# A two-layer encoder trunk: solved diagonal blocks sent through DRAM in other pieces, the block step's operands and a decay strip made in another order, and own buffers for a reload

## The chip, the cores and the metric

The kernel runs on one core of a Trainium2 chip. The metric is the device time of one launch in microseconds (us). Three runs of the kernel before took 2922.13 us in the median (2919.28 to 2929.7).

## What is computed

Two layers over 528 tokens (16 learned ones and 512 given) of 1024 channels, all in float32. Each layer normalises its input, projects it with one wide matrix, and mixes the tokens in two ways: a gated delta rule with 8 heads of 128 channels, and a retention with 4 heads of 256/512 channels, each run forwards and backwards. Both results are normalised per head, gated, projected up, merged with sigmoid gates, projected, and added to the residual; a SwiGLU network follows. The part that the change touches is the delta rule, whose chunks need a triangular system solved:

```python
m = jnp.einsum('nbhid,nbhjd->nbhij', kb, k) * decay * lower_strict
a = m + jnp.eye(CHUNK, dtype=m.dtype)
u = lax.linalg.triangular_solve(a, v * beta[..., None], left_side=True, lower=True, unit_diagonal=True)
w = lax.linalg.triangular_solve(a, kb * jnp.exp(gc)[..., None], left_side=True, lower=True, unit_diagonal=True)
```

and the retention's decay factors, a power of the distance between two tokens, `exp(rel * log_gamma)`.

## The kernel before, in words

**Matrix work.** `project` (L422) and its generator `units` loop over tiles of 128 output columns. A weight tile of 1024 x 128 (512 KB) is loaded by a DMA (`wraw`, three buffers), split into a rounded part by ScalarE (`whi`, L178) and a rest by VectorE (`wlo`, L179; four buffers each), and multiplied in three passes (`mm3`): 48 matrix products for the two halves of 264 tokens. In the last layer most products need only the 512 given tokens.

**Two streams.** Per layer there are four groups of two delta-rule heads. `gdn_begin` projects q, k and v of a group; `gdn_chain` then solves and scans it. `weave` mixes `gdn_chain`, which is a chain of small steps, with `filling`: retention heads 0 to 2 and gate projections, which keep TensorE busy. When the fourth group's chain runs, the filling ends; retention head 3 and the last gates are traced behind it.

**The solve.** For each head and direction (four per group, `j`) `gdn_products` makes `N`, 4 chunks of 128 x 128 with the chunk's tokens on the partitions (for direction 1 its transpose `NT`). The 32 x 32 diagonal blocks are wanted one per partition: `N` is written whole to a DRAM tile `nd` (L617), and four DMAs (L622) gather 4 blocks each, in pieces of 128 bytes, into 16 partitions of `w0` (called `w` in the profile). The meta tokens' block goes the same way through `ndm` (L624, L625). `gdn_solve` (L646) then inverts all 68 blocks at once on VectorE: 30 steps of a product (`st`) and a sum (`w`). The result is written to the DRAM tile `xd` in one DMA of 68 rows of 4 KB (L660).

**The block step.** `gdn_levels` (L664), once per head, reads its blocks back as `qc` with 128 partitions (L679), copies and transposes them in blocks of 32 (ScalarE L689, L690, L695; VectorE L686), and spreads them over block-diagonal tiles: `T` and `Q` (both `QT` in the profile) and `TT` by VectorE, `Qf` and `Qb` by ScalarE (L125). TensorE's first product `lvy` needs `T`; its next, `lvt`, needs `Q` and the masked result `Y`. Small products for blocks of 64 follow, then the scan `gdn_scan`.

**The decay strip.** `retention` (L933) loads a strip of distances (L936), makes the decay factors on VectorE (`su`, `strip`) and ScalarE (`Exp`), projects q and k, rotates them (`rot`, `ru`), lets its `filler` run, and multiplies the first scores with the strip (`pr`).

**The reload.** After the last scan `load_a` (L1130) reads back, per head, the delta rule's output (`lo<-od_a`), its gate (`lz<-zd`) and a row of inverse roots (`rs<-rsd`), 264 KB each, multiplies them and splits the result (`oh`, `ol`) for the up-projection. All three tiles come from `ctmp`, a ring of six buffers. `load_b` does the same for the retention with the same ring.

**Order.** All data DMAs are issued by SP, in one queue, and an issue that has to wait holds up those behind it. The order of the instructions on each engine is made by a planner: it walks the traced program by priority, with a simulated timeline. `tc.high_priority(offset=...)` moves what is inside ahead: weights by 200 (`PRI`), `load_a` by 1000 (`OA`), `load_b` by 300 (`OB`). The numbers given to `yield` are the shares by which `weave` mixes the streams. On the chip every engine follows its own list in order.

Of the kernel before, what the change touches and what calls it, by code (L numbers as in the profile page):

```python
# [9 lines left out]
F32 = mybir.dt.float32  # L10
F32R = mybir.dt.float32r
I32 = mybir.dt.int32
AF = mybir.ActivationFunctionType
# [5 lines left out]
P = 128  # L19
# [4 lines left out]
L = NM + SEQ  # L24
NC = 4
# [8 lines left out]
SW = L + 400  # L34
# [58 lines left out]
def bc(ap, shape):  # L93
    return ap.to_broadcast(shape)
# [305 lines left out]
def layer(tc, nc, env, l, xn, gd):  # L400
# [124 lines left out]
    def tok(c):  # L525

        return (NM + c * P, P) if c < NC else (0, NM)
# [44 lines left out]
    def gdn_products(h, st):  # L572
        s = st[h]
        hh = h % 2
        q, k = s["q"], s["k"]
        kk, kq, km = ct("kk"), ct("kq"), ct("km")
        for c in range(NCH):
            n0, n = tok(c)
            a = kk[:, c * P:(c + 1) * P] if c < NC else km[0:NM, 0:NM]
            b = kq[:, c * P:(c + 1) * P] if c < NC else km[0:NM, NM:2 * NM]  # L580
            mm(a, k[:, n0:n0 + n], k[:, n0:n0 + n])
            mm(b, k[:, n0:n0 + n], q[:, n0:n0 + n])
        yield 0.4
        s["gr"], s["N"], s["P"], s["Pm"] = [], [], [], []
        cn = st["cn"]
        for d in range(2):
            gr = gp.tile([P, L], F32, name="gcr", tag="gcr", bufs=4)
            nc.sync.dma_start(gr, grow[d * 8 + h:d * 8 + h + 1, :].partition_broadcast(P))
            dd = tp.tile([P, NC, P], F32, name="dd", tag="u", bufs=UB)
            dm = gp.tile([NM, NM], F32, name="dm", tag="dm", bufs=2)  # L590
            mk = cst["maskF"] if d == 0 else cst["maskB"]
            for c in range(NCH):
                n0, n = tok(c)
                o = dd[:, c] if c < NC else dm
                stt(o, gr[0:n, n0:n0 + n], gc[0:n, d, c, h:h + 1], mk[0:n, 0:n], SUB, MIN)
            act(dd, dd, AF.Exp)
            act(dm, dm, AF.Exp)
            yield 1.6
            N = gp.tile([P, NC, P], F32, name="N", tag="NQ", bufs=8)
            Nm = gp.tile([32, 32], F32, name="Nm", tag="Nm", bufs=4)  # L600
            nc.vector.memset(Nm, 0.0)
            Pt = gp.tile([P, NC, P], F32, name="P", tag="P", bufs=4)
            Pm = gp.tile([NM, NM], F32, name="Pm", tag="Pm", bufs=6)
            for c in range(NC):
                stt(N[:, c], kk[:, c * P:(c + 1) * P], cn[:, d, c, hh:hh + 1], dd[:, c], MUL, MUL)
            stt(Nm[0:NM, 0:NM], km[0:NM, 0:NM], cn[0:NM, d, NC, hh:hh + 1], dm, MUL, MUL)
            yield 1.3

            j = hh * 2 + d
            src, srcm = N, Nm  # L610
            if d == 1:
                src = tp.tile([P, NC, P], F32, name="NT", tag="u", bufs=UB)
                nc.vector.transpose(src.rearrange("p c d -> p (c d)"), N.rearrange("p c d -> p (c d)"))
                srcm = gp.tile([32, 32], F32, name="NmT", tag="NmT", bufs=2)
                nc.vector.transpose(srcm, Nm)
            nd = dp.tile([P, NC, P], F32, name="nd", tag="nd", bufs=8)
            nc.sync.dma_start(nd, src)  # L617
            w0 = st["w0"]
            for c in range(NC):
                base = nd[:, c, :]  # L620
                blocks = bass.AP(base.tensor, base.offset, [[32 * NC * P + 32, 4], [NC * P, 32], [1, 32]])
                nc.sync.dma_start(w0[j * 16 + c * 4:j * 16 + c * 4 + 4, :].rearrange("b (r i) -> b r i", r=32), blocks)  # L622
            ndm = dp.tile([32, 32], F32, name="ndm", tag="ndm", bufs=8)
            nc.sync.dma_start(ndm, srcm)  # L624
            nc.sync.dma_start(w0[64 + j:65 + j, :], ndm.rearrange("r i -> (r i)").unsqueeze(0))  # L625
            tt(Pt.rearrange("p c d -> p (c d)"), kq, dd.rearrange("p c d -> p (c d)"), MUL)
            tt(Pm, km[0:NM, NM:2 * NM], dm, MUL)
            s["gr"].append(gr)
            s["N"].append(N)
            s["P"].append(Pt)  # L630
            s["Pm"].append(Pm)
            yield 1.2
# [15 lines left out]
    def gdn_solve(st):  # L648
        w0 = st["w0"]
        w3 = w0.rearrange("p (r i) -> p r i", r=32)  # L650
        nc.gpsimd.memset(w0[:, 0:1024:33], 1.0)
        for q in range(30, 0, -1):
            n = 31 - q
            t = gp.tile([68, 256], F32, name="st", tag="sc", bufs=SB)[:, :q * n].rearrange("p (j i) -> p j i", j=q)
            tt(t, bc(w3[:, 0:q, q:q + 1], [68, q, n]), bc(w3[:, q:q + 1, q + 1:32], [68, q, n]), MUL)
            tt(w3[:, 0:q, q + 1:32], w3[:, 0:q, q + 1:32], t, ADD)
            if q % 2:
                yield 1.05
        xd = dp.tile([68, 1024], F32, name="xd", tag="xd", bufs=2)
        nc.sync.dma_start(xd, w0)  # L660
        st["xd"] = xd
        yield 4.0

    def gdn_levels(h, st):  # L664
# [4 lines left out]
        xd = st["xd"]  # L669
# [5 lines left out]
        qf, tb = comp[:, 0], comp[:, 1]  # L675
        for d, t in enumerate((qf, tb)):
            j = hh * 2 + d
            base = xd[j * 16:j * 16 + 16, :]
# [4 lines left out]
        tm, qm, tl, qb = more[:, 0], more[:, 1], last_[:, 0], last_[:, 1]  # L683

        def turn(o, a, p0, p1):
            nc.vector.transpose(fl(o)[p0:p1], fl(a)[p0:p1])  # L686


        nc.scalar.copy(tm, tb)  # L689
        nc.scalar.copy(qm, qf)  # L690
        for p0 in (0, 64):
            turn(tm, qf, p0, p0 + 32)
            turn(qm, tb, p0, p0 + 32)

        nc.scalar.copy(tl[64:128], tb[64:128])  # L695
        turn(tl, qf, 0, 64)
        turn(qb, tb, 0, P)

        def spread(o, a, m, n):
            tt(o.rearrange("p c (b i) -> p c b i", b=n), bc(a.unsqueeze(2), [P, NC, n, 32]),  # L700
               bc(m.unsqueeze(1).unsqueeze(3), [P, NC, n, 32]), MUL)

        T, Q, Qf, Qb = (gp.tile([P, NC, P], F32, name=n, tag="NQ", bufs=8) for n in ("QT", "QT2", "Qf", "Qb"))
        TT = gp.tile([P, NC, 64], F32, name="TT", tag="sc", bufs=SB)
        spread(T, tm, cst["bm"], 4)
        spread(Q, qm, cst["bm"], 4)
        spread(TT, tl, cst["bm2"], 2)
        for o, a in ((Qf, qf), (Qb, qb)):
            for b in range(4):
                act(o[:, :, b * 32:b * 32 + 32], a, AF.Copy, scale=cst["bm"][:, b:b + 1])  # L710
# [22 lines left out]
        lo, hi = slice(0, 64), slice(64, 128)  # L733
# [129 lines left out]
    def sums(ps):  # L863

        while later:
            later.pop(0)(ps)
# [66 lines left out]
    def retention(h, filler):  # L933
        strip = rp.tile([P, SW], F32, name="strip", tag="strip")
        o0 = COFF["rel"][0]
        nc.sync.dma_start(strip, constd[:, o0:o0 + SW])  # L936
        for a0 in (0, SW // 2):
            sl = slice(a0, a0 + SW // 2)
            u = tmp("su")[:, 0:SW // 2]
            ts(u, strip[:, sl], lgn[:, 8 * l + 4 + h:8 * l + 5 + h], MUL)  # L940
            stt(strip[:, sl], strip[:, sl], lg[:, 8 * l + h:8 * l + h + 1], u, MUL, MIN)
        act(strip, strip, AF.Exp)
        tt(strip[:, 400:400 + P], strip[:, 400:400 + P], ident, ADD)
        rot = []
        for s, (c0, hv) in enumerate(((C_QB, tail), (C_KB, FULL))):
            pre = [tmp("rp0"), tmp("rp1")]
# [4 lines left out]
            r = rp.tile([P, 2, L], F32, name="rot", tag="rot", bufs=2)  # L951
            u = tmp("ru")
            sl = slice(hv[0][0], L)
# [4 lines left out]
            u = tmp("ru")  # L958
# [3 lines left out]
            rot.append(r)  # L962
        q, k = rot
        sums(pt)
        yield from filler
        pr = []

# [148 lines left out]
    bp = bctx.enter_context(tc.tile_pool(name=f"bp{l}", bufs=1, reuse_waits="tile"))  # L1116

    def spread(row):
        r = ctmp("rs")
        nc.sync.dma_start(r[:, t0:L], rsd[row:row + 1, :].partition_broadcast(P))  # L1120
        return r
# [8 lines left out]
    def load_a():  # L1130
        inverse_roots(0, 8)
        res = []
        for h in range(H):
            o, z, rs = ctmp("lo"), ctmp("lz"), spread(h)
            nc.sync.dma_start(o[:, t0:L], od_a[h, :, t0:L])
            nc.sync.dma_start(z[:, t0:L], zd[h, :, t0:L])
            stt(o[:, t0:L], o[:, t0:L], gain[:, 40 + l:41 + l], rs[:, t0:L], MUL, MUL)
            tt(o[:, t0:L], o[:, t0:L], z[:, t0:L], MUL)
            res.append(split_tile(o))
        return [x[0] for x in res], [x[1] for x in res]  # L1140
# [32 lines left out]
    for i in range(8):  # L1173
# [9 lines left out]
        b = xp.tile([P, L], F32R, name="xl", tag="xl", bufs=8)  # L1183
# [99 lines left out]
    for i in range(FT):  # L1283
# [3 lines left out]
        a, b = split_tile(ff[i], i < 9)  # L1287
# [3 lines left out]
    if not last:  # L1291
        nrm = Norm(8 * (l + 1), FULL)
        hs = residual(w_ffn_out[l], (8, 8, 6), (fh, fl_), True, nrm.add, nrm.ready, lambda: nrm.root(0), 1, LF)
        r = boundary(nrm, hs, lambda xs, two, **kw: first_gates(l + 1, xs, two, **kw))
# [75 lines left out]
```

## Time and profile before

| | kernel before |
|---|---|
| median of three runs | 2922.13 us |
| lowest, highest | 2919.28, 2929.7 us |
| the profiled execution | 2919.6 us |
| its span, first to last instruction | 2917.7 us |
| mean granted TensorE clock | 0.987 |
| moved by DMAs, mean rate | 313.48 MB, 107 GB/s |

The span is 1.9 us shorter than the profiled execution's own time. Busy times are in us; PE is TensorE, DVE VectorE, ACT ScalarE, SPq the queue of SyncE, which issues the DMAs. Time stamps count from the first instruction. The part of the profile that follows the chain of work back from the last instruction tells what released each step; a wait is put down to the releaser that came last. A granted clock of 1.00 is 2.4 GHz, 0.50 is 1.2 GHz.

### The profile page before, as it was taken

The numbers are of one execution on the slowest core, as the hardware profiler recorded it, in microseconds if no ns is written. First come the engines' busy times: TensorE is split into PE (matmuls) and PEld (weight loads), VectorE is DVE, ScalarE is ACT, GpSimd is POOL, SyncE is SP. The second block draws the span as 40 slices with busy tenths as digits, with TensorE's granted clock in tenths as the row PEclk, the third lists the DMA queues.
The fourth block names the chain that finished last, engine by engine and source line by source line (L and its number), as shares of the span: only waits on it lengthen the run. The fifth ranks groups of instructions, "written<-read, shape, count | busy, mean of one in ns | idle before, by whom it ended". The sixth has DMA issues, their size and how long they took to land.

```text
span 2917.7 us, 48775 instructions
## 1 busy us (share of the span) xinstructions
PE 2822.1 (97%) x19487; PEld 2579.0 (88%) x19487; DVE 1795.2 (62%) x3854; ACT 1101.0 (38%) x2171; POOL 9.0 (0%) x114
## 2 busy tenths in 40 slices
PE   8999999999999999999999999999997999999998
PEld 8999999999889999999999888888886788888887
DVE  6877858768664545343258779687786564543433
ACT  5444445345333233222234344453443332332222
POOL 0000000000000000000000000000000000000000
PEclk9999999999899999999999999999998999999999
DMA  5433323324245442333444423334241464433332
GB/s 166 112 83 83 100 77 85 99 74 125 70 145 171 137 143 84 91 89 99 123 116 112 107 71 108 88 94 106 71 140 44 154 192 125 130 109 94 92 110 80
DMA packets 506423, 313.48 MB, mean 107 GB/s; under 512 B 55633, under 2 KB 460779, under 8 KB 506195
## 3 DMA queue, kind: packets, MB, share of 16 engines
q1 hardware_dynamic: 506194, 310.36, 37.1%
q8 instruction: 153, 2.51, 0.4%
q14 instruction: 76, 0.61, 0.1%
HBM read 265.28 MB, written 45.02 MB: 106 GB/s over the span
## 4 chain that ended last, share of the span: by engine, by line
PE 84%; DVE 8%; DMA 5%; ACT 2%; issue 1%; SPq 0%; DVEq 0%; ACTq 0%
PE mmps L112 67%; PE rpv L112 3%; PE fu L112 2%; PE oo L112 2%; PE sn L112 1%; DVE wlo L179 1%; PE yy L112 1%; DMA xd<-w 1%; PE ks L112 1%; DMA lo<-od_a 1%; PE rs L112 1%; PE lvy L112 1%; PE lvt L112 1%; DMA lo<-od_b 1%; PE lvq L112 1%
## 5 line engine op out<-in xcount | busy, mean ns | idle before, releaser
L112 PE MATMUL mmps<-xh,whi 128*128 128x264 f32 (+1 forms) x3840 | 1188.0, 310 | 23.7 <-DVE rg L115 12.4
L112 PE MATMUL mmps<-xl,whi 128*128 128x264 f32 (+1 forms) x3840 | 1179.5, 308 | 0.0
L112 PE MATMUL mmps<-xh,wlo 128*128 128x264 f32 (+1 forms) x3808 | 1173.3, 308 | 0.0
L112 PEld LDWEIGHTS mmps<-xh,whi 128*128 128x128 f32 x3840 | 727.2, 189 | 63.2 <-DVE rg L115 14.6
L178 ACT CAST whi<-wraw 128x1024 fp32r<-128x1024 f32 (+1 forms) x392 | 407.3, 1040 | 991.2 <-PE mmps L112 737.0
L179 DVE TENSOR_TENSOR wlo<-wraw,whi 128x1024 fp32r<-128x1024 f32 (+1 forms) x392 | 474.4, 1210 | 485.3 <-ACT whi L178 484.4
L112 PEld LDWEIGHTS mmps<-xl,whi 128*128 128x128 f32 x3840 | 726.2, 189 | 37.0 <-issue 2.9
L112 PEld LDWEIGHTS mmps<-xh,wlo 128*128 128x128 f32 x3808 | 719.9, 189 | 34.3 <-issue 0.5
L112 PE MATMUL mmps<-oh,whi 128*128 128x264 f32 (+2 forms) x1126 | 358.5, 319 | 0.0
L112 PE MATMUL mmps<-oh,wlo 128*128 128x264 f32 (+2 forms) x1126 | 358.1, 318 | 0.0
L112 PE MATMUL mmps<-ol,whi 128*128 128x264 f32 (+2 forms) x1126 | 357.3, 318 | 0.5 <-DVE ol L179 0.4
L112 PEld LDWEIGHTS mmps<-ol,whi 128*128 128x128 f32 x1126 | 211.6, 188 | 16.4 <-DVE ol L179 0.9
L112 PEld LDWEIGHTS mmps<-oh,wlo 128*128 128x128 f32 x1126 | 211.7, 188 | 15.7 <-issue 0.2
L112 PEld LDWEIGHTS mmps<-oh,whi 128*128 128x128 f32 x1126 | 211.5, 188 | 15.0
L115 DVE SCALAR_TENSOR_TENSOR ac<-xc,cw,ac 128x528 f32<-128x528 f32 x192 | 143.6, 759 | 3.4 <-ACT ac L125 0.6
L118 DVE TENSOR_TENSOR ff<-fg,mmps 128x264 f32<-128x264 f32 (+1 forms) x63 | 32.5, 516 | 116.0 <-PE mmps L112 116.0
L112 PE MATMUL rpv<-prh,rv 128*128 128x264 f32 (+1 forms) x384 | 95.5, 323 | 0.0
L118 DVE TENSOR_TENSOR st<-w 68x30 f32<-68x30 f32 (+14 forms) x240 | 78.2, 326 | 19.0 <-DMA w<-ndm 7.1
L118 DVE TENSOR_TENSOR w<-w,st 68x30 f32<-68x30 f32 (+14 forms) x240 | 78.2, 326 | 6.8
L125 ACT ACTIVATE gth<-mmps 128x264 f32<-128x264 f32 (+1 forms) x132 | 59.8, 454 | 57.4 <-PE mmps L112 57.4
L112 PE MATMUL rs<-rot 128*128 128x264 f32 (+3 forms) x240 | 75.1, 456 | 2.8 <-DVE z L115 2.4
L115 DVE SCALAR_TENSOR_TENSOR hn<-mmps,hold 128x264 f32<-128x264 f32 (+2 forms) x51 | 25.4, 498 | 82.6 <-PE mmps L112 76.5
(315 smaller groups left out, 3216.3 us busy)
## 6 DMA issues: line engine op xcount, KB each, us to landing
wraw<-in_w_in_dram SPq DMA_DIRECT2D x194, 512.0 KB
wraw<-in_w_ffn_in_dram SPq DMA_DIRECT2D x88, 512.0 KB
wraw<-in_w_up_b_dram SPq DMA_DIRECT2D x32, 512.0 KB
wraw<-in_w_ffn_out_dram SPq DMA_DIRECT2D x32, 512.0 KB
gcr<-grow SPq DMA_DIRECT2D x32, 264.0 KB
wraw<-in_w_up_a_dram SPq DMA_DIRECT2D x16, 512.0 KB
wraw<-in_w_out_dram SPq DMA_DIRECT2D x16, 512.0 KB
wraw<-in_w_ffn_out_dram SPq DMA_DIRECT2D x16, 384.0 KB
```

What stands on the lines that cost most here:

```text
L112: newest[0] = nc.tensor.matmul(o, lhsT=l, rhs=r, start=start, stop=stop)
L115: (eng or nc.vector).scalar_tensor_tensor(out=o, in0=a, scalar=s, in1=b, op0=op0, op1=op1)
L118: (eng or nc.vector).tensor_tensor(out=o, in0=a, in1=b, op=op)
L125: nc.scalar.activation(o, a, f, **kw)
L178: a = nc.scalar.copy(hi, src)
L179: return a.ins, nc.vector.tensor_tensor(out=lo, in0=src, in1=hi.bitcast(F32), op=SUB).ins
```

## The change

Five edits. The diagonal blocks alone are written to DRAM, by four DMAs, in the order in which `w0` wants them, and come back in one DMA of 16 rows. The solved blocks are written to `xd` by two DMAs, 64 rows and 4 rows. In the block step `T` is made as soon as its transposes are done, and what `Q`, `TT` and `qb` need comes after. The decay strip's arithmetic stands behind the projections of q and k instead of ahead of them; its load stays. In the reload `lo` gets eight buffers of its own (`mrg`, which the gated products use later).

```diff
@@ -613,13 +613,12 @@
-            nd = dp.tile([P, NC, P], F32, name="nd", tag="nd", bufs=8)
-            nc.sync.dma_start(nd, src)
+            nd = dp.tile([16, 1024], F32, name="nd", tag="nd", bufs=8)
+            for b in range(4):
+                o = slice(b * 32, b * 32 + 32)
+                nc.sync.dma_start(bass.AP(nd.tensor, nd.offset + b * 1024, [[32, 32], [4096, NC], [1, 32]]), src[o, :, o])
             w0 = st["w0"]
-            for c in range(NC):
-                base = nd[:, c, :]
-                blocks = bass.AP(base.tensor, base.offset, [[32 * NC * P + 32, 4], [NC * P, 32], [1, 32]])
-                nc.sync.dma_start(w0[j * 16 + c * 4:j * 16 + c * 4 + 4, :].rearrange("b (r i) -> b r i", r=32), blocks)
+            nc.sync.dma_start(w0[j * 16:j * 16 + 16, :], nd)
@@ -657,7 +656,8 @@
         xd = dp.tile([68, 1024], F32, name="xd", tag="xd", bufs=2)
-        nc.sync.dma_start(xd, w0)
+        nc.sync.dma_start(xd[0:64], w0[0:64])
+        nc.sync.dma_start(xd[64:68], w0[64:68])
@@ -685,26 +685,26 @@
-        nc.scalar.copy(tm, tb)
-        nc.scalar.copy(qm, qf)
-        for p0 in (0, 64):
-            turn(tm, qf, p0, p0 + 32)
-            turn(qm, tb, p0, p0 + 32)
-
-        nc.scalar.copy(tl[64:128], tb[64:128])
-        turn(tl, qf, 0, 64)
-        turn(qb, tb, 0, P)
...
+        nc.scalar.copy(tm, tb)
+        for p0 in (0, 64):
+            turn(tm, qf, p0, p0 + 32)
         spread(T, tm, cst["bm"], 4)
+        nc.scalar.copy(qm, qf)
+        for p0 in (0, 64):
+            turn(qm, tb, p0, p0 + 32)
         spread(Q, qm, cst["bm"], 4)
+
+        nc.scalar.copy(tl[64:128], tb[64:128])
+        turn(tl, qf, 0, 64)
         spread(TT, tl, cst["bm2"], 2)
+        turn(qb, tb, 0, P)
@@ -934,13 +934,6 @@
         nc.sync.dma_start(strip, constd[:, o0:o0 + SW])
-        for a0 in (0, SW // 2):
-            sl = slice(a0, a0 + SW // 2)
-            u = tmp("su")[:, 0:SW // 2]
-            ts(u, strip[:, sl], lgn[:, 8 * l + 4 + h:8 * l + 5 + h], MUL)
-            stt(strip[:, sl], strip[:, sl], lg[:, 8 * l + h:8 * l + h + 1], u, MUL, MIN)
-        act(strip, strip, AF.Exp)
-        tt(strip[:, 400:400 + P], strip[:, 400:400 + P], ident, ADD)
         rot = []
@@ -962,6 +955,13 @@
         q, k = rot
         sums(pt)
+        for a0 in (0, SW // 2):
...
+        tt(strip[:, 400:400 + P], strip[:, 400:400 + P], ident, ADD)
         yield from filler
@@ -1131,7 +1131,7 @@
-            o, z, rs = ctmp("lo"), ctmp("lz"), spread(h)
+            o, z, rs = bp.tile([P, L], F32, name="lo", tag="mrg", bufs=8), ctmp("lz"), spread(h)
```

The lines that the fifth hunk adds and that are left out here are those that it removes above, unchanged.

## Rows read from the trace of the kernel before

**Rows 1.** The page's first part: busy us (share of the span) and instructions.
```profile
PE 2822.1 (97%) x19487; PEld 2579.0 (88%) x19487; DVE 1795.2 (62%) x3854; ACT 1101.0 (38%) x2171; POOL 9.0 (0%) x114
```

**Rows 2.** The page's fourth part: the chain that ended last, shares of the span by line.
```profile
PE mmps L112 67%; PE rpv L112 3%; PE fu L112 2%; PE oo L112 2%; PE sn L112 1%; DVE wlo L179 1%; PE yy L112 1%; DMA xd<-w 1%; PE ks L112 1%; DMA lo<-od_a 1%; PE rs L112 1%; PE lvy L112 1%; PE lvt L112 1%; DMA lo<-od_b 1%; PE lvq L112 1%
```

**Rows 3.** Waits of TensorE: waiting for, us in total, times, longest us.
```profile
PE lvy L112 <- DVE QT L118: 21.4, 6, 10.4
PE mmps L112 <- DVE rg L115: 12.4, 8, 4.2
```

**Rows 4.** Timeline of TensorE: start us, us, what, count [idle before <-releaser].
```profile
189.72 0.49 PE L112 MATMUL lvy<-QT,N 128*128 128x128 f32 x2 [0.81 <-DVE QT L118]
...
381.49 0.59 PE L112 MATMUL mmps<-xh,whi 128*128 128x264 f32 x1 [3.34 <-DVE ro L118]
...
578.87 1.01 PE L112 MATMUL lvy<-QT,N 128*128 128x128 f32 x3 [2.63 <-DVE QT L118]
...
763.02 1.16 PE L112 MATMUL lvy<-QT,N 128*128 128x128 f32 x8 [1.43 <-DVE QT L118]
...
775.42 0.98 PE L112 MATMUL lvy<-QT,N 128*128 128x128 f32 x3 [3.04 <-DVE QT L118]
...
2215.39 2.08 PE L112 MATMUL lvy<-QT,N 128*128 128x128 f32 x8 [10.42 <-DVE QT L118]
...
2227.93 2.08 PE L112 MATMUL lvy<-QT,N 128*128 128x128 f32 x8 [3.04 <-DVE QT L118]
```

**Rows 5.** The chain in order of time behind layer 1's fourth solve: start us, us, what.
```profile
2202.62 6.12 DMA xd<-w
...
2209.17 2.13 DMA qc<-xd
```

**Rows 6.** Timeline of VectorE in the same stretch.
```profile
2211.39 0.62 DVE L686 STREAM_TRANSPOSE qd<-qc 32x128 f32<-32x128 f32 x2 [3.42 <-DMA qc<-xd]
...
2214.65 1.29 DVE L118 TENSOR_TENSOR QT<-qd,c_bm 128x512 f32<-128x512 f32 x2
```

**Rows 7.** Busy time by stretch; the first row names the columns.
```profile
core 0: us, PE busy (x) PEld busy (x) DVE busy (x) ACT busy (x) POOL busy (x), PEclk, DMA share, GB/s
...
2204.20:2208.60 4.40, 0.77 (x5) 0.20 (x3) 2.46 (x3) 1.80 (x3) 0.00 (x0) 1.00 0.21 67
380.30:387.10 6.80, 5.61 (x25) 5.61 (x26) 4.22 (x10) 3.34 (x12) 0.00 (x0) 0.50 0.35 111
578.30:581.70 3.40, 2.83 (x13) 2.83 (x14) 2.38 (x4) 2.37 (x6) 0.00 (x0) 0.50 0.22 65
772.90:783.10 10.20, 6.90 (x38) 6.41 (x39) 4.16 (x11) 2.30 (x9) 0.00 (x0) 0.50 0.05 15
2209.90:2223.50 13.60, 7.32 (x40) 6.68 (x40) 5.72 (x14) 4.21 (x14) 0.00 (x0) 0.50 0.30 58
...
831.00:866.00 35.00, 31.09 (x219) 27.63 (x219) 29.62 (x49) 15.90 (x30) 0.00 (x0) 1.00 0.78 241
```

**Rows 8.** The chain in order of time before layer 0's first solve.
```profile
138.55 2.44 DMA nd<-NT
...
142.11 2.09 DMA w<-nd
```

**Rows 9.** Issues of SP: start us, us of the issue, what, count.
```profile
318.41 0.32 SPq L624 DMA_DIRECT2D ndm<-Nm  x1
...
320.23 0.23 SPq L625 DMA_DIRECT2D w<-ndm  x1
```

**Rows 10.** Groups of instructions: busy us, mean ns | idle before, releasers with us.
```profile
L118 DVE TENSOR_TENSOR st<-w 68x30 f32<-68x30 f32 (+14 forms) x240 | 78.2, 326 | 19.0 <-DMA w<-ndm 7.1 <-DMA w<-nd 5.8
...
L115 DVE SCALAR_TENSOR_TENSOR lo<-lo,gain,rs 128x528 f32<-128x528 f32 (+1 forms) x16 | 12.2, 760 | 9.5 <-DMA lo<-od_a 9.4
```

**Rows 11.** Timeline of VectorE inside layer 1's fourth solve.
```profile
2181.13 0.82 DVE L122 TENSOR_SCALAR su<-strip,lgn 128x464 f32<-128x464 f32 x2
...
2182.18 0.69 DVE L115 SCALAR_TENSOR_TENSOR strip<-strip,lg,su 128x464 f32<-128x464 f32 x1
```

More of the change, by code (lines that the diff above doesn't have):

```diff
@@ L964, in retention @@
         sums(pt)
+        for a0 in (0, SW // 2):
+            sl = slice(a0, a0 + SW // 2)
+            u = tmp("su")[:, 0:SW // 2]
+            ts(u, strip[:, sl], lgn[:, 8 * l + 4 + h:8 * l + 5 + h], MUL)
+            stt(strip[:, sl], strip[:, sl], lg[:, 8 * l + h:8 * l + h + 1], u, MUL, MIN)
+        act(strip, strip, AF.Exp)
+        tt(strip[:, 400:400 + P], strip[:, 400:400 + P], ident, ADD)
         yield from filler
```

## The prediction

> **What bounds the kernel now.** I read the page first for the engines: TensorE is busy for 97% of the span [rows 1], and the chain that ended last runs for 67% through the matrix products of `mmps`, while `xd<-w` and `lo<-od_a` have about 1% each [rows 2]. So almost all of the time is matrix work that the change leaves alone; only what TensorE spends idle, or at half its clock, can be won. The waits of TensorE say where that is: its longest is for `QT`, the first operand of the block step (`lvy`), 21.4 us in six waits, then 12.4 us in eight for `rg`, a result of VectorE that stands behind other things in its queue [rows 3]. The third reading is TensorE's timeline around the eight solves. Seven waits belong to them, five in layer 0 and two in layer 1 [rows 4]: in the first three groups of layer 0 (0.81, 3.34, 2.63 us), and in the fourth group of either layer, where little other matrix work is left, one for each of the two heads (1.43 and 3.04; 10.42 and 3.04). The first three groups of layer 1 have none.
>
> What they wait for is in the chain of the last group: the solve ends, `xd<-w` takes 6.12 us, `qc<-xd` 2.13 us [rows 5], then VectorE starts its transposes at 2211.39 and the two `QT` products at 2214.65 [rows 6]. VectorE had stood still for 3.42 us in front of the transposes. In group two of layer 0 TensorE's wait is for `ro` [rows 4], an ordinary product behind that same standstill.
>
> The granted clock is read from stretches: after such a wait TensorE runs at 0.50 of its full clock, the 1.2 GHz level instead of 2.4, for 6.8 us, 3.4 us, 10.2 us and 13.6 us at the four places listed [rows 7]. Work done there takes twice as long.
>
> **The change part by part.** All terms are against the profiled execution, 2919.6 us (span 2917.7); the median of the three runs, 2922.1, stands 2.5 us above it, and I add that at the end.
>
> *xd as 64 and 4 rows* (eight times). The 68 rows move 67 GB/s with a DMA share of 0.21 while they are under way [rows 7], about 3.4 of 16 engines: the transfer is slow because few engines carry it. A tile of 256 KB over 128 rows lands in 2.44 us where nothing is ahead of it [rows 8]. I take 2.9 us for the new pair (2.44, and a second issue of about the 0.3 that an issue takes [rows 9]) instead of 6.12, a gain of 3.2. Bounds: 2.44 and 6.12. The Trainium skill ("DMA: Bandwidth & Descriptors", Why a DMA increments its semaphore by 16 and not by 1) gives the engines as the largest number up to 16 that divides the outer dimensions: 4 for 68 rows, 16 for 64. The share of 0.21 agrees with four. The same page (Rules for kernel authors) advises against splitting a transfer by partitions, since both parts use the same engines; by that rule alone nothing would be won here, and it is the first rival.
> What reaches TensorE is the gain or the wait, whichever is smaller [rows 4]: 3.2 of 3.34, 2.6 of 2.63, 0.8 of 0.81, 1.4 of 1.43, 3.2 of 10.42. **-11.2 us**; bounds -12 and 0. In layer 1's first three groups it is worth nothing, since TensorE has no wait there.
>
> *T first.* Today VectorE does six transposes, two rotary products and `TT` before the first `QT` ends; from 2211.39 to 2214.65 plus half of 1.29 that is 3.9 us [rows 6]. After the change two transposes (0.62) and one product (0.65) stand ahead of `lvy`, 1.3 us: a gain of 2.6 at the wait of 10.42. At the two waits of 3.04 [rows 4] copies for the head before lie in between, so I take 1.8 each. The rest (`Q`, `TT`, `qb`) then runs beside `lvy`, and is next in line to be late: `lvt` needs `Q`. **-6.2 us**; bounds -7.8 and 0 (if the order on VectorE stays as it is).
>
> *The clock.* If the waits of 3.34 and 2.63 go, so does the half clock behind them: half of 5.61 and of 2.83 us of work, 4.2. In the two last groups 6.90 and 7.32 us are worked at half clock [rows 7]; waits remain there, so I take a third of the 7.1 to be had. **-6.6 us**; bounds -11.3 and 0.
>
> *Diagonal blocks alone.* Seven DMAs before (one tile, four gathers, two for the meta block), seven after (four block pieces, one load, the same two). The old path is 2.44 for the tile, then three more issues, then 2.09 for the last gather [rows 8]; the new one is four issues, a landing of the same kind, one issue and a landing. Equal within 0.5 us, and SP waits once in either, with the weight loads queued behind that wait. The solve now waits 12.9 us in all for these loads (7.1 and 5.8) [rows 10]. **0**; bounds -2 and +18 (second rival). What hides it is the work of the other stream; without it the solve starts later by as much.
>
> *Strip late* (eight times). The strip's products on VectorE (0.82, and twice 0.69) lie in the middle of the fourth group's solve in layer 1 [rows 11]. The solve is a chain on VectorE, so its end moves forward by about 2 us in layer 1, where TensorE waits for it. The products go to the wait for `qc`, in which VectorE stands for 3.42 us anyway [rows 6]. The strip's own load stays where it was. **-2 us**; bounds -4 and +3 (if they get in front of the first scores instead).
>
> *Own reload buffers.* VectorE waits 9.4 us for `lo<-od_a` [rows 10]; three heads instead of two can now be under way. But the stretch has a DMA share of 0.78 at 241 GB/s and VectorE is busy for 29.62 of 35 us [rows 7], so little can move. TensorE's waits here are among those for `rg` [rows 3]. **-3 us**; bounds -9.4 and +34 (last rival). The eight `mrg` buffers are next wanted for the gated products after the first up-projection, by which time the reload is read: nothing.
>
> *The new order.* Instructions are ordered by a planner that starts anew; a few waits will appear elsewhere. Three of the size of those for `rg` (12.4 in 8, 1.5 each [rows 3]): **+4.6 us**; bounds 0 and +15.
>
> Sum: -11.2 - 6.2 - 6.6 + 0 - 2 - 3 + 4.6 = -24.4, so 2895.2 in the profiled execution and **2898 us** beside the median.
>
> **The rivals.** About 0.5% (14.6 us) is what a measurement of this kernel can tell from no change, so faster begins under 2907.5.
> *The split of xd wins nothing* (both pieces stay behind the weight loads, or the readers wait for both as long as before, so that the change doesn't do what it says). Against it is the share of 0.21 [rows 7]; for it, that all transfers go through SP's one queue, behind weight tiles of 512 KB. Then the terms for xd and the clock go: 2898 + 17.8 = 2916. Chance 0.13.
> *Short writes.* The blocks now go to DRAM in pieces of 128 bytes instead of 2 KB. If four pieces landed as late as `xd` does today (6.12 instead of 2.44), eight solves would start 3.7 us later; the two last groups and layer 0's other three would pass that on, 18 us: 2916. Against it: `ndm`, pieces of 128 bytes too, was sent at 318.41 and its reader was issued at 320.23 [rows 9], so it had landed within 1.8 us. The Trainium skill (the same page, Specifications) says that transfers below 512 bytes are read, modified and written; by that rule this rival would be the likelier; the trace's 1.8 us shows no such price, though for 32 pieces only. Chance 0.08.
> *The new order eats it.* Ten new waits of 1.5 instead of three: 2898 + 10.9 = 2909. Chance 0.10.
> *The reload pushes out the weights* (the slower side). The reload's loads and products are planned far ahead of everything else; with buffers of their own, nothing holds them back any more. The place is the stretch after the last group's scan. Its 24 transfers of 264 KB are 6.3 MB, 26 us at 241 GB/s. If they all went first, TensorE would have one weight tile in hand, 48 of the 219 matrix products that take 31.09 us there [rows 7], 6.8 us; it would stand for 19 us instead of the 3.9 of now, and 1.5 more at half clock: 16.8 a layer, 34 in all, and the 3 us gained there are lost: 2935. It decides the sign from 11 us a layer on. For it: a DMA share near 0.8; against: today's buffers already let two heads go ahead, and loads of weights still came between. Chance 0.07.
>
> **How the numbers follow.** The forecast has 0.62. Faster: 0.60 of that, and the parts of the third and first rival that stay under 2907.5 (0.05 and 0.03): 0.68. Slower by over 0.5%: the last rival, 0.07. The rest, 0.25, is within it. The low end takes four fifths of the 22 us that the lower bounds (-46.5 in all) leave under the sum: 2880; the high end takes in the first two rivals: 2917.
>
> **What would show it.** Right: `xd` landing under 3.5 us in the chain; the wait of 10.42 down to 2 to 5; those of 3.34 and 2.63 gone with the half clock behind them; about 1.3 us from the first transpose to `lvy`; no strip products inside the solve. Wrong: `xd` still near 6 us; blocks landing after more than 4 us; a wait for `rg` or for weights longer than 4.2 in the reload; more idle time of TensorE outside the solves than 5 us over what is there now.

## The result, and the profile after

The changed kernel takes 2910.89 us in the median of six runs (2908.56 to 2912.14), the kernel before beside it 2927.46 us (six runs, 2919.28 to 2931.21). The ratio is 0.9943, with a 95% interval of 0.9931 to 0.9955: faster by 0.57%. The profiled execution took 2910.8 us, its span 2909.0.

The profile after answers to [rows 1, 2] with these lines of the page: the engines do the same work, and `xd<-w` and `lo<-od_a` are no longer among the largest shares of the chain that ended last.

```profile
PE 2824.6 (97%) x19487; PEld 2581.4 (89%) x19487; DVE 1795.3 (62%) x3854; ACT 1101.5 (38%) x2171; POOL 9.4 (0%) x114
...
PE mmps L112 69%; PE rpv L112 3%; PE fu L112 2%; PE oo L112 2%; PE sn L112 1%; PE yy L112 1%; PE rs L112 1%; DVE wlo L179 1%; PE ks L112 1%; DMA lo<-od_b 1%; DMA gcr<-grow 1%; PE lvy L112 1%; PE lvt L112 1%; PE l64b L112 0%; PE l L112 0%
```

The waits of TensorE after (waiting for, us in total, times, longest us), beside [rows 3]:

```profile
PE lvy L112 <- DVE QT L118: 11.1, 4, 6.1
...
PE mmps L112 <- DVE rg L115: 8.2, 8, 2.7
...
PE rvm L1011 <- DVE pr L118: 5.8, 2, 2.9
```

The first two fell by 14.5 us together; the third, for the product of scores and strip (`pr`), is new among the longer ones. The timeline of TensorE after shows where they lie:

```profile
152.91 0.28 PE L1011 MATMUL rvm<-c_ident,rvc 128*16 128x128 f32 x1 [2.93 <-DVE pr L118]
...
773.92 2.05 PE L112 MATMUL lvy<-QT,N 128*128 128x128 f32 x8 [6.08 <-DVE QT L118]
...
2208.56 1.16 PE L112 MATMUL lvy<-QT,N 128*128 128x128 f32 x8 [0.31 <-DVE QT L118]
...
2218.80 2.05 PE L112 MATMUL lvy<-QT,N 128*128 128x128 f32 x8 [3.52 <-DVE QT L118]
```

Against [rows 4], the wait of 10.42 is down to 0.31, and those of 0.81, 2.63 and 1.43 are gone (3.34 is now 1.19). But one of 2.93 stands at the first solve, and the second head of layer 0's fourth group waits 6.08 where it waited 3.04. The chain of the last group in order of time, beside [rows 5]:

```profile
2199.65 3.38 DMA xd<-w
...
2203.47 2.23 DMA qc<-xd
```

From the issue of `xd` to that of `qc` it is 2.87 to 3.4 us in seven solves and 4.13 in one; before it was 4.9 to 6.2. In the last group a weight tile is still under way when the pair is issued, so the pair is read by itself behind layer 0's third solve: 178 GB/s at a DMA share of 0.80 (67 and 0.21 for the whole in [rows 7]). The other stretches show the half clock gone at the two places of layer 0's second and third group:

```profile
core 0: us, PE busy (x) PEld busy (x) DVE busy (x) ACT busy (x) POOL busy (x), PEclk, DMA share, GB/s
...
572.10:573.60 1.50, 1.50 (x15) 1.50 (x14) 0.00 (x0) 1.07 (x2) 0.00 (x0) 1.00 0.80 178
...
153.30:160.00 6.70, 5.44 (x24) 5.44 (x25) 6.30 (x18) 1.73 (x4) 0.00 (x0) 0.50 0.29 81
...
380.30:387.10 6.80, 5.61 (x47) 5.32 (x47) 5.83 (x12) 4.76 (x16) 0.00 (x0) 1.00 0.42 119
578.30:581.70 3.40, 3.40 (x31) 3.40 (x30) 2.69 (x5) 2.47 (x7) 0.00 (x0) 1.00 0.52 141
```

Instead, 6.7 us at half clock stand behind the new wait at the first solve. VectorE's timeline in the last group, beside [rows 6], is the line that tells most about the forecast:

```profile
2205.79 0.61 DVE L686 STREAM_TRANSPOSE qd<-qc 32x128 f32<-32x128 f32 x2 [0.41 <-DMA qc<-xd]
2206.44 0.50 DVE L686 STREAM_TRANSPOSE qe<-qc 64x128 f32<-64x128 f32 x2
2206.87 0.57 DVE L686 STREAM_TRANSPOSE qd<-qc 32x128 f32<-32x128 f32 x2
2207.47 0.43 DVE L118 TENSOR_TENSOR TT<-qe,c_bm 128x256 f32<-128x256 f32 x1
2207.81 1.29 DVE L118 TENSOR_TENSOR QT<-qd,c_bm 128x512 f32<-128x512 f32 x2
```

All six transposes and `TT` still stand ahead of both `QT` products, as before, and so it is in all 16 heads of the trace after. The text of the kernel put `T` first; the planner's list for VectorE did not. From the first transpose to the end of the first `QT` it is 2.7 us here, where it was 3.9 with two sums of the rotary in between [rows 6]. Layer 0's first solve is later, and VectorE's timeline shows what now stands ahead of it:

```profile
122.03 1.30 DVE L115 SCALAR_TENSOR_TENSOR strip<-strip,lg,su 128x464 f32<-128x464 f32 x2
...
143.08 0.69 DVE L613 STREAM_TRANSPOSE NT<-N 128x512 f32<-128x512 f32 x1
...
151.03 0.20 DVE L118 TENSOR_TENSOR st<-w 68x30 f32<-68x30 f32 x1 [4.67 <-DMA w<-nd]
```

The strip's products of the first retention head are now among the products that make group one's `N`. The same steps in VectorE's timeline before:

```profile
47.04 0.70 DVE L115 SCALAR_TENSOR_TENSOR strip<-strip,lg,su 128x464 f32<-128x464 f32 x1
...
137.02 0.69 DVE L613 STREAM_TRANSPOSE NT<-N 128x512 f32<-128x512 f32 x1
...
144.42 0.20 DVE L118 TENSOR_TENSOR st<-w 68x30 f32<-68x30 f32 x1 [1.16 <-DMA w<-ndm]
```

The last `NT` is 6.1 us later, and the solve that waits for it 6.6. The strip is not all of it: with the strip early again (e3 in the table below) the changed kernel's first solve is still 3.3 us late, and by which edit is open. The strip of the last head of layer 1 now runs behind the whole block step:

```profile
2256.03 1.31 DVE L115 SCALAR_TENSOR_TENSOR strip<-strip,lg,su 128x464 f32<-128x464 f32 x2
```

The new path of the blocks, in the chain before that solve (beside [rows 8]), has landings of the old size:

```profile
146.06 2.81 DMA nd<-NT
...
148.95 1.96 DMA w<-nd
```

From the first issue for the last `NT` to the solve it is 6.5 us, with the four pieces in SP's issues at 144.49, and before it was 5.9 (138.55 to 144.42):

```profile
144.49 2.00 SPq L619 DMA_DIRECT2D nd<-NT  x4
```

The waits of VectorE for the solve's blocks and for the reload, beside [rows 10]:

```profile
L118 DVE TENSOR_TENSOR st<-w 68x30 f32<-68x30 f32 (+14 forms) x240 | 78.2, 326 | 14.2 <-DMA w<-nd 8.2
L118 DVE TENSOR_TENSOR lo<-lo,rs 128x528 f32<-128x528 f32 (+1 forms) x32 | 21.3, 697 | 12.8 <-DMA lo<-od_b 12.8
L115 DVE SCALAR_TENSOR_TENSOR lo<-lo,gain,rs 128x528 f32<-128x528 f32 (+1 forms) x16 | 12.1, 758 | 6.0 <-DMA lz<-zd 5.2 <-DMA rs<-rsd 0.8
```

The wait for `lo<-od_a` is gone, but 5.2 us of it are now for `lz`, the next tile of the same load, which kept the ring of six buffers.

The two profiled executions differ by 8.8 us (that of before, 2919.6 us, is near the low end of its runs). Where these come from is read by following the same instruction through the traces. The table gives, for the profiled execution of each kernel, how much later (+) or earlier (-) than before that instruction starts: the first product of layer 0's first solve; the first up-projection product of layer 0 (the end of its mixing); the first product of layer 1's fourth solve; the first `lvy` there; the first up-projection product of layer 1; the first output product. The kernels are those of the next section.

| | first solve | layer 0 mixed | 4th solve, layer 1 | its lvy | layer 1 mixed | output |
|---|---|---|---|---|---|---|
| before starts at | 144.42 | 895.96 | 2163.02 | 2215.39 | 2339.40 | 2811.53 |
| after | +6.6 | +0.8 | +3.2 | -6.8 | -8.7 | -8.6 |
| e1: blocks by the old path | +7.2 | -0.9 | +2.6 | -6.2 | -3.0 | -1.5 |
| e2: xd whole | +5.9 | +7.9 | +10.8 | +3.5 | +4.3 | +3.2 |
| e3: strip early | +3.3 | -6.1 | -4.8 | -8.5 | -8.9 | -8.9 |
| e4: reload from the ring | +6.7 | +1.2 | +3.5 | -6.8 | -6.4 | -7.8 |
| f1: xd alone | +0.5 | -9.7 | -6.6 | -10.1 | -9.5 | -9.4 |
| f3: strip alone | +6.1 | +4.9 | +6.2 | -0.4 | +0.9 | +1.0 |
| f4: lo alone | +0.6 | +0.7 | +1.9 | +1.4 | +4.6 | +5.0 |
| h1: strip late in the last head | +2.8 | -6.6 | -6.4 | -16.4 | -17.3 | -16.0 |
| f2: T tied | +5.7 | -11.1 | -11.3 | -22.4 | -24.3 | -24.2 |
| h2: both | +1.1 | -10.0 | -8.6 | -19.1 | -20.4 | -18.8 |

So layer 0 gained nothing, and the whole gain was made in layer 1's last group, 10.0 us of it in the 52 us from the start of its solve to `lvy`: 6.1 in the solve (from its first product to the issue of `xd`, 39.6 us before and 33.5 after), 2.7 from there to the issue of `qc`, 1.1 from there to `lvy`. Each column can be read as a difference to its neighbour; a single execution can lie some 7 us off the median of its kernel, so verdicts rest on the medians and ratios, and places on the table, as one execution of each kernel shows them.

### The profile page after: what moved, and what is told of

Its sections match the earlier page's. It is cut to its first block, busy times and chain, and to the rows that moved or that the text cites. A ratio compares the mean times of both kernels' runs of the same rounds, so it can differ in the third digit from the quotient of the medians.

```text
span 2909.0 us, 48823 instructions
## 1 busy us (share of the span) xinstructions
PE 2824.6 (97%) x19487; PEld 2581.4 (89%) x19487; DVE 1795.3 (62%) x3854; ACT 1101.5 (38%) x2171; POOL 9.4 (0%) x114
## 4 chain that ended last, share of the span: by engine, by line
PE 87%; DVE 6%; DMA 3%; ACT 1%; issue 1%; SPq 1%; DVEq 0%; ACTq 0%
PE mmps L112 69%; PE rpv L112 3%; PE fu L112 2%; PE oo L112 2%; PE sn L112 1%; PE yy L112 1%; PE rs L112 1%; DVE wlo L179 1%; PE ks L112 1%; DMA lo<-od_b 1%; DMA gcr<-grow 1%; PE lvy L112 1%; PE lvt L112 1%; PE l64b L112 0%; PE l L112 0%
```

## The experiments

Unless it says otherwise, each is the changed kernel with one part undone or altered; ratios are to the kernel before on the same chip, whose medians were 2922 to 2924 us.

**e1, the blocks by the old path.**

```diff
...
-            for b in range(4):
-                o = slice(b * 32, b * 32 + 32)
-                nc.sync.dma_start(bass.AP(nd.tensor, nd.offset + b * 1024, [[32, 32], [4096, NC], [1, 32]]), src[o, :, o])
+            nc.sync.dma_start(nd, src)
...
```

> The changed kernel with the diagonal blocks sent the old way (whole tile to DRAM, four gathers). Theory: the four block issues per head and direction lengthen SP's list in layer 0's first group, so its solve starts 6.6 us later than before and TensorE waits 3.2 + 1.6 us there; undone, the solve starts at about 144.5 us again instead of 151.0 and the kernel takes 5 to 8 us less than the changed one (2911), about 2904. Rival: the late start comes from the newly planned order as a whole, not from the blocks; then the first solve still starts at 149 to 152 us and the time stays within 3 us of the changed kernel.

2914.03 us (2912.9 to 2917.83), ratio 0.9965 [0.9953, 0.9977]. The first solve starts 7.2 us later than before, as in the changed kernel (6.6): the late start is not the blocks' doing. The 3 us more in the median (6 by the ratios) are barely told apart, since the intervals overlap; in the profile, the slowest of the six executions, they arise behind the last group's first `lvy`. Two waits, of 1.71 and 2.42 us, stand there, and TensorE is at half clock for the 30 us that follow, in which it waits 3.33 us more for the second head:

```profile
2209.19 1.16 PE L112 MATMUL lvy<-QT,N 128*128 128x128 f32 x8 [1.71 <-DVE QT L118]
...
2212.77 2.08 PE L112 MATMUL lvt<-Y,QT 128*128 128x128 f32 x8 [2.42 <-DVE Y L118]
...
core 0: us, PE busy (x) PEld busy (x) DVE busy (x) ACT busy (x) POOL busy (x), PEclk, DMA share, GB/s
2211.40:2242.00 30.60, 25.12 (x138) 21.84 (x139) 13.09 (x36) 8.70 (x28) 0.00 (x0) 0.50 0.10 22
```

**e2, the solved blocks in one DMA.**

```diff
-        nc.sync.dma_start(xd[0:64], w0[0:64])
-        nc.sync.dma_start(xd[64:68], w0[64:68])
+        nc.sync.dma_start(xd, w0)
```

> The changed kernel with xd written in one DMA of 68 rows again. Theory: the split is the larger part of the gain; xd lands in 5 to 6.2 us again instead of 3.2 to 3.4, the waits for the block step in layer 0's second and third group and in the last group come back, and the kernel takes 8 to 13 us more than the changed one, 2919 to 2924. Rival (the gain comes from the new order and from the strip, the transfer is hidden): within 4 us of 2911.

2920.55 us (2916.42 to 2924.53), ratio 0.9991 [0.9982, 0.9999]. Without the split nearly all of the gain is gone. In the issues of SP the reader is 6.19 us behind the write again:

```profile
2207.26 0.28 SPq L659 DMA_DIRECT2D xd<-w  x1
2213.45 0.92 SPq L678 DMA_DIRECT2D qc<-xd  x2
```

**e3, the strip early again** (its arithmetic back behind its load, in all heads).

```diff
         nc.sync.dma_start(strip, constd[:, o0:o0 + SW])
+        for a0 in (0, SW // 2):
...
```

> The changed kernel with the strip's arithmetic back ahead of the projections. Theory: the fourth solve of layer 1, 33.5 us from the first st to xd in the changed kernel and 39.6 before, becomes 2.5 to 6 us longer, and so does the wait behind it: 2913 to 2917. Rival: the solve is shorter for another reason; then it stays near 33.5 us and the time within 2 us of 2911.

2909.2 us (2904.14 to 2910.76), ratio 0.9947 [0.9934, 0.9959]: the same as the changed kernel. The table shows that this is no "nothing": layer 0 ends 6.9 us earlier than with the late strip, and from the fourth solve of layer 1 to its `lvy` 6.3 us of that are lost.

**e4, the reload from the ring.**

```diff
-            o, z, rs = bp.tile([P, L], F32, name="lo", tag="mrg", bufs=8), ctmp("lz"), spread(h)
+            o, z, rs = ctmp("lo"), ctmp("lz"), spread(h)
```

> The changed kernel with lo taken from the ring of six again. Theory: the own buffers let the reload run closer together, which cost as much in layer 0 (waits of 3.1 and 1.5 us before rvm and mmps at 849 to 854 us, half clock behind them) as they won in layer 1 (wait of 2.9 instead of 4.5): within 3 us of 2911. Rival 1 (they win what was forecast): 3 to 6 us more. Rival 2 (they push out the weights in layer 0): 5 us less, and the waits at 849 to 854 us gone.

2911.64 us (2908.51 to 2916.4), ratio 0.996 [0.9948, 0.9973]. Up to the reload it runs like the changed kernel within 0.4 us; at the reload's end it is 0.4 us later in layer 0 and 2.4 in layer 1, and 0.8 at the output. By the ratio it is 5 us behind the changed kernel, by the median 0.8; the intervals overlap.

**f1, the kernel before with the split of xd alone.** The diff is that of e2, turned round.

> The kernel before with xd written in 64 and 4 rows and nothing else changed. Theory: this edit alone carries the gain; xd lands in 3.2 to 3.4 us, the waits of 3.3 and 2.6 us in layer 0's groups two and three and the half clock behind them go, the wait of 10.4 in the last group falls by about 3: 9 to 14 us less than before, ratio 0.995 to 0.997. Rival (it needs the other edits to reach TensorE): ratio 0.998 or more.

2909.36 us (2904.32 to 2910.26), ratio 0.9949 [0.9935, 0.9962]. One line makes as much as all five edits. It gains in layer 0, where the changed kernel gains nothing. TensorE's waits are those that the term for `xd` named: 0.81, 3.34, 2.63 and 1.43 of layer 0 are gone, and 10.42 is 3.2 shorter:

```profile
2205.32 1.01 PE L112 MATMUL lvy<-QT,N 128*128 128x128 f32 x3 [7.20 <-DVE QT L118]
```

**f2, the changed kernel with the order on VectorE tied**: the other transposes and products may be issued only after `T`'s product.

```diff
-        spread(T, tm, cst["bm"], 4)
+        first = spread(T, tm, cst["bm"], 4)
...
+        with tc.issue_after(first):
+            for p0 in (0, 64):
+                turn(qm, tb, p0, p0 + 32)
+            spread(Q, qm, cst["bm"], 4)
...
```

> The changed kernel with VectorE's list tied so that the product for T really stands behind its two transposes (in the changed kernel the planner put it behind all six and TT in all sixteen heads). Theory: from the first transpose to the first lvy it is 1.3 to 1.8 us instead of 2.6 to 8.7; the waits of 6.1 us (layer 0) and 3.5 us (layer 1) for the second heads of the last groups fall by 2 to 4 us each; 4 to 6 us less than the changed kernel, 2905 to 2907, ratio about 0.9925. Rival: lvt then waits for Q instead, and the time stays within 2 us of the changed kernel's.

2902.17 us (2895.19 to 2905.0), ratio 0.9926 [0.9912, 0.994]. VectorE's timeline in the last group now has the order that the change meant:

```profile
2190.71 0.61 DVE L686 STREAM_TRANSPOSE qd<-qc 32x128 f32<-32x128 f32 x2 [0.48 <-ACT qd L695]
2191.36 0.69 DVE L689 TENSOR_TENSOR QT<-qd,c_bm 128x512 f32<-128x512 f32 x1
2191.97 0.61 DVE L686 STREAM_TRANSPOSE qd<-qc 32x128 f32<-32x128 f32 x2
```

`QT` ends 1.34 us after the first transpose starts. Of the table's -24 the median confirms -20; the profiled execution was the quickest of its six. The gain over the changed kernel does not lie where it was forecast: by the table 11.9 of 15.6 us are there at the end of layer 0, and 1.1 are made from the last solve's start to its `lvy`. Some 6 of them are the clock: half clock, summed from the granted clock of 5 us stretches, is 52.2 us against 64.8 in the changed kernel. In layer 0's fourth group the wait of 6.08 is gone, and one of 3.27 stands at the next product:

```profile
771.09 1.16 PE L112 MATMUL lvt<-Y,QT 128*128 128x128 f32 x8 [3.27 <-DVE Y L118]
```

**f3, the kernel before with the late strip alone.**

```diff
-        for a0 in (0, SW // 2):
...
         sums(pt)
+        for a0 in (0, SW // 2):
...
```

> The kernel before with the strip's arithmetic late in every head and nothing else. Theory (late costs some 3 to 4 us before the first solve in layer 0, and is worth something in the last group only where the solved blocks land early): 2923 to 2928 us, ratio 1.000 to 1.002, the first solve 3 to 4 us later than in the kernel before. Rival (late is worth its 2 us or more in the last group of each layer by itself, as forecast): 2916 to 2920 us, ratio 0.998 to 0.999.

2923.36 us (2920.46 to 2928.51), ratio 0.9999 [0.999, 1.0008]. It is two opposite things: the first solve is 6.1 us late, and that is the late strip's work by itself; then layer 1's fourth solve and block step win 6.6 of it back. VectorE's timeline in layer 0 is that of the changed kernel again:

```profile
121.54 1.29 DVE L115 SCALAR_TENSOR_TENSOR strip<-strip,lg,su 128x464 f32<-128x464 f32 x2
...
150.55 0.20 DVE L118 TENSOR_TENSOR st<-w 68x30 f32<-68x30 f32 x1 [4.51 <-DMA w<-ndm]
```

**f4, the kernel before with the own reload buffers alone.** The diff is that of e4, turned round.

> The kernel before with own reload buffers and nothing else. Theory (worth 0 to 3 us): 2919 to 2924 us, ratio 0.999 to 1.000; the waits before the merges at the end of each layer fall by about 2 us. Rival (the earlier reloads stand in front of the weights on the queue and give TensorE a new wait): 2926 to 2935 us.

2924.93 us (2920.69 to 2931.89), ratio 1.0009 [0.9999, 1.0019]. Worth nothing that can be measured; the last rival's 34 us are excluded.

**h1, the strip late in the last head alone.**

```diff
+        def decays():
...
+        if h < RH - 1:
+            decays()
...
         sums(pt)
...
+        if h == RH - 1:
+            decays()
```

> The changed kernel with the strip late for the last retention head only, early for the other three. Theory: late strips of heads 0 to 2 cost, because head 0's falls among the products ahead of the first solve, which started 6.6 us later; that of head 3 wins, because it leaves the last solve. The first solve starts at 145 to 148 us, the last solve takes about 33.5 us, and the kernel takes 4 to 8 us less than the changed one, 2903 to 2907, ratio about 0.992. Rival: the planned order shifts the waits about at random; then within 3 us of 2911 with the first solve's start unchanged.

2898.26 us (2897.36 to 2903.41), ratio 0.992 [0.9907, 0.9932]. By the ratios this is some 7 us better than the changed kernel, with intervals that just touch. Heads 0 to 2 keep layer 0's gain, head 3 keeps the last group's (10.0 us from the last solve's start to `lvy`). TensorE's wait there:

```profile
2198.95 1.16 PE L112 MATMUL lvy<-QT,N 128*128 128x128 f32 x8 [0.25 <-DVE QT L118]
```

**m1, xd as 34 and 34 rows** (a single run).

```diff
-        nc.sync.dma_start(xd[0:64], w0[0:64])
-        nc.sync.dma_start(xd[64:68], w0[64:68])
+        nc.sync.dma_start(xd[0:34], w0[0:34])
+        nc.sync.dma_start(xd[34:68], w0[34:68])
```

> The changed kernel with xd written as two pieces of 34 rows. If the number of engines by the outer dimension sets the time (34 divides by 2 only), the pieces run on two engines each and xd lands in 8 to 10 us, later than the 5 to 6.2 of one piece; if it is two transfers in place of one that wins, xd lands in 3 to 4 us as with 64 and 4.

One run, 2918.38 us. The issues of SP in the last group:

```profile
2202.58 0.26 SPq L659 DMA_DIRECT2D xd<-w  x1
2202.89 0.28 SPq L660 DMA_DIRECT2D xd<-w  x1
2207.49 0.93 SPq L679 DMA_DIRECT2D qc<-xd  x2
2210.14 0.32 SPq L750 DMA_DIRECT2D Qm<-xd  x1
```

`qc` of the first head reads rows 0 to 31, the first piece, and waits 4.91 us for half the bytes. `Qm` reads the meta rows in the second piece, and is issued 7.25 us after it and 2.65 us behind `qc` (1.0 in the kernels before and after, where all of `xd` has landed by then). Once the weight tile ahead of them is through, the two pieces move 52 GB/s at a DMA share of 0.13, about 2 of 16 engines:

```profile
2204.70:2208.40 3.70, 3.70 (x33) 3.70 (x32) 2.46 (x3) 1.32 (x2) 0.00 (x0) 1.00 0.13 52
```

Two pieces of equal size end later than one whole (5 to 6.5 us), though less late than expected. So it is not two transfers in place of one that gains; the shares of 0.21, 0.80 and 0.13 go with the row counts.

**h2, h1 and f2 together.**

> The changed kernel with both repairs: the strip's arithmetic late in the last head alone, and the transposed block product tied to come directly after its own two transposes. Theory (the two lie in different places: the strip of head 0 ahead of group one's first scores in layer 0, the transposed product at the head of every solve and above all of the last): their gains over the changed kernel (2902.17 and 2898.26 against 2910.89, so 8.7 and 12.6 us) add for the most part: 2888 to 2894 us, ratio to before 0.989 to 0.991, the wait before the first product of the transposed solve in the last group near zero. Rival (both gains are the same one, the half clock of the last group that either of them happens to prevent): 2896 to 2902 us, no better than the better of the two.

2897.93 us (2895.57 to 2901.77), ratio 0.9916 [0.9903, 0.9929]. The rival's time is right: no better than h1 (0.992). Its cause, the half clock of the last group, is not shown. What the record shows is that little was left to win where the term put it: the wait before `lvy` in the last group, 0.25 us in h1, is zero, as expected, and TensorE waits just behind it instead:

```profile
2196.32 1.05 PE L112 MATMUL lvy<-QT,N 128*128 128x128 f32 x8
2198.27 1.16 PE L112 MATMUL lvt<-Y,QT 128*128 128x128 f32 x8 [0.90 <-DVE Y L118]
```

In layer 0 the table has h2 3.4 us ahead of h1, and f2 1.1 ahead of h2; the medians of h1 and h2 are the same.

**i1, the kernel before with the split of xd and `T` tied.** The edit puts f2's lines in place of the three old products, but leaves the old copies and transposes standing above them, so these are made twice in every head. It doesn't answer the question that was put to it.

```diff
         turn(tl, qf, 0, 64)
         turn(qb, tb, 0, P)
...
+        nc.scalar.copy(tm, tb)
+        for p0 in (0, 64):
+            turn(tm, qf, p0, p0 + 32)
+        first = spread(T, tm, cst["bm"], 4)
...
```

> The kernel before with the solved blocks sent as 64 and 4 rows and the transposed block product tied behind its own two transposes; diagonal blocks, strip and reload buffers as before. Theory (the pair of moves that shorten one stretch are what counts, the three others are about nothing together): 8 us under the kernel with the 64 and 4 rows alone (2909.36), so 2898 to 2904 us, ratio 0.992 to 0.994. Rival (the tied product gains only beside the other changes): 2907 to 2912 us.

2920.31 us (2915.28 to 2927.57), ratio 0.9988 [0.9979, 0.9997], 11 us above f1. Read for what it is, it prices needless work at this place: the page has VectorE busy for 1820.6 us where f1's has 1796.6, and with these 24.0 us of transposes (and some 11 us of copies on ScalarE, 1113.7 against 1102.3) the kernel is 11 us slower, although VectorE is idle for 38% of the span and `T` is tied. How much the tie gives back in this is not told apart. In the last group `T`'s product starts 3.58 us after the first transpose, behind other transposes and two sums of the rotary:

```profile
2212.37 0.61 DVE L687 STREAM_TRANSPOSE qd<-qc 32x128 f32<-32x128 f32 x2 [0.61 <-DMA qc<-xd]
...
2215.29 0.62 DVE L687 STREAM_TRANSPOSE qd<-qc 32x128 f32<-32x128 f32 x2
2215.95 0.69 DVE L701 TENSOR_TENSOR QT<-qd,c_bm 128x512 f32<-128x512 f32 x1
```

Whether the split and the tied `T` do better alone than h1 was not tried, nor the split with the strip late in the last head.

## Why the forecast held, and where its steps did not

The sign came out, and two thirds of the size (0.9943 against a forecast of 24.4 us less, which is 0.9916), at the slow end of the range. What held is the term for `xd`. That the total stayed in the range is in part luck: the terms for `T`, the strip and the reload, 11.2 us together, brought nothing that can be told from zero, and the 4.6 us set aside for the new order and the width of the range made up for them.

- **xd as 64 and 4 rows** (-11.2): right, and nearly the whole result. The landing of 2.9 us was forecast and 2.87 to 3.4 measured in seven solves. In one solve it was 4.13. Alone (f1) it is worth 13 us; taken away (e2) it leaves 0.1%. In layer 0 it gives -9.7 with the clock, where the four waits and the clock had been put at -8 and -4.2. In the last group, where 3.2 more were forecast, f1 has the `lvy` 3.5 us earlier against the start of the solve, but is only 2.8 better at the end. The first rival (the split wins nothing) fell. The rule behind it in the Trainium skill ("DMA: Bandwidth & Descriptors", Rules for kernel authors) is about two halves that each spread over all 16 engines; the 68 rows, at a share of 0.21, did not, so it does not carry over to them. The same page's rule of the largest divisor (Why a DMA increments its semaphore by 16 and not by 1; 4 for 68, 16 for 64, 2 for 34) agrees with all three shares, 0.21, 0.80 and 0.13: 34 rows by that rule are 17 rows to an engine, as 68 are, and the first piece took 4.91 us against 5 to 6.5.
- **The clock** (-6.6): right in layer 0's second and third group. Over the span, the half clock summed from the granted clock of 5 us stretches is 71.5 us before and 64.8 after, so 3.4 us of time, half of the term. The term counted the half clock that goes and none that comes: new half clock came up at the first solve and in layer 0's reload stretch, 7 us at either. In f1 the same sum is 75.2 us, so `xd` alone gave none back over the span.
- **T first** (-6.2): this step failed. I took "After the change two transposes (0.62) and one product (0.65) stand ahead of `lvy`" from the order of the text; the bound of zero, "if the order on VectorE stays as it is", is what happened: in all 16 heads six transposes and `TT` stand ahead, and in the last group it is 2.7 us from the first transpose to the end of the first `QT`, not 1.3. Whether the order pays as forecast stays open. Tied (f2), it gives 8.7 us by the medians and 5 by the ratios (0.9926 against 0.9943, intervals that overlap a little), near the 6.2, but in the profile it does so in layer 0 and in part through the clock, not at the wait of 10.42; beside h1 it gives nothing (h2). That the wait of 10.42 fell to 0.31 nonetheless was xd and the strip: the stretch from the solve's start to `lvy` got 10.0 us shorter, and alone it is 3.5 in f1 and 6.6 in f3.
- **Strip late** (-2): the wrong size at both places, and the wrong sign at one. The step that failed is "The products go to the wait for `qc`": they do so in none of the eight heads. The last head's run at 2256.03, some 50 us behind that wait. The first head's go in front of group one's blocks, the case of the upper bound, and cost 4.9 us by the end of layer 0 (f3), not 3 in all. Out of the last solve the products are gone, as forecast, but that is worth more than their own 2.2 us: in f3 the solve is 35.2 us from its first product to the issue of `xd`, 39.6 before, and the stretch up to `lvy` 6.6 shorter. By the end of layer 1's mixing 5.3 of that are left (from +6.2 to +0.9), and 3.9 over layer 1 as a whole (from +4.9). In sum nothing (0.9999).
- **Diagonal blocks** (0): right by their landings, 2.81 and 1.96 us where the old were 2.44 and 2.09, and 0.6 us longer as a whole path (6.5 against 5.9); e1 has the same first solve. Whether they are worth nothing in the whole kernel is open: taking them back costs 3 us by the medians and 6 by the ratios, beyond the bound of -2, with intervals that just overlap. The second rival, short writes that land late, is excluded by the 2.81; the Trainium skill's note (the same page, Specifications) on transfers below 512 bytes has no visible price here.
- **Own reload buffers** (-3): too much. f4 says 1.0009, e4 puts it at 0.4 to 2.4 us. The wait moved on to `lz`.
- **The new order** (+4.6): too little in layer 0. After is 10.5 us worse than f1 there (+0.8 against -9.7). The strip explains about 5 (f3) to 7 (e3); the remaining 3 to 5 are the size forecast, and a part of them is the second head's wait of 6.08 instead of 3.04. Which of the remaining edits moved that order is open.

The parts that were run alone add up within their intervals: f1, f3 and f4 multiply to 0.9957, the whole change is 0.9943.

## What to carry to other kernels

A transfer that feeds a waiting chain should have a row count that spreads over many DMA engines (here a share of 0.21 for 68 rows, 0.80 for 64 and 4); where a few rows are left over, send them by themselves: this was one line and nearly the whole gain. A statement moved in the source is no move until the engine's own timeline shows it, and the same edit can help in one place of a loop and harm in another (the strip: +4.9 and -3.9), so it is worth asking of each iteration who stands behind the moved work. A total of zero may hide two effects that can be had apart: late only where it helps took the ratio from 0.9943 to 0.992, some 7 us.

## What was not expected of the hardware

The scatter of the kernel before goes with its granted clock: of 56 runs on three chips, the 15 with a mean of 0.983 took 2926.1 us on average, the 13 with 0.985 2923.0, and the 4 with 0.987 2918.6. So the times of one program differ by some 7 us along with the share of the span in which TensorE is held at 1.2 GHz, and a single profile can stand that far from the median (i1's is the slowest of its runs, f2's the quickest); what sets that share in a run is not shown. In e1 waits of 1.71 and 2.42 us were followed by 30 us at that level, with TensorE busy for 25.12 of them and one more wait of 3.33 in between. And two transfers of 34 rows, half the bytes each, could be read hardly sooner than one of 68: after 4.91 us the first, after 7.25 the second.
